# The feed-forward of a hybrid decoder layer: eight quarter products, or seven with sums and differences kept in DRAM

## The chip, the cores and the metric

The kernel runs on one core of a Trainium2 chip. The metric is the device time of one execution in microseconds. A core has five engines that each work through their own queue in order: TensorE (PE in the profile, with its weight loads as PEld), VectorE (DVE), ScalarE (ACT), GpSimd (POOL) and SyncE (SP). SP issues most DMAs, GpSimd a few. They meet through semaphores: an instruction that waits holds up all that stands behind it on its engine.

## What is computed

One layer on 2048 prompt tokens and 32 sample tokens, all in float32: an input projection, dilated attention and a gated branch, an output projection with norms, and then a feed-forward with a squared ReLU. The change is about the last part:

```python
x = x + rms_norm(merged @ w_out, norm_post_mix)
h2 = rms_norm(x, norm_pre_ffn)
f = jnp.square(jax.nn.relu(h2 @ w_up)) @ w_down      # 1024 -> 4096 -> 1024
x = x + rms_norm(f, norm_post_ffn)
```

## The kernel before

**Tokens.** The work is done in two spans, one after the other: span 0 has 1024 prompt and the 32 sample tokens (1056), span 1 has 1024. For each span the loop at the end of `hybrid_step` runs six projections with attention, `gmlp`, `mix`, the output projection (`out_and_norms` for span 0, `out_rows` for span 1) and `ffn`.

**Products.** A float32 number is held as two parts, high and low, in a format that TensorE takes at full rate. A product of two such numbers is three matrix instructions: high by high, high by low, low by high (L247 in `gemm`, L261 in `gemm_rows`). `load_w` fetches 512 KB of a weight from DRAM into `raw` (L218, on SP), ScalarE makes the high part (L234), GpSimd the low part by a subtraction (L237; every second one goes to VectorE while `share[0]` is set). The pool `wp` holds two buffers each of `raw`, `wh` and `wl`, so a weight's parts can be made once TensorE has done with the weight two before. The six 128-column weights of the first two attention steps are called weight 1 to 6 below, in the order in which their subtractions stand on GpSimd; 1 and 2 are q and k of the first step.

**Feed-forward.** `ffn` goes through the 32 row blocks of `w_up`: `up` makes one block for all tokens of the span, in tiles of 352 columns (span 0) or 512 (span 1), then ReLU on ScalarE, the square on VectorE, and the split in two parts. After each four blocks `down` or `down_rows` multiplies them by the matching part of `w_down` and VectorE adds the result to an accumulator in SBUF (L1106, L1118). For span 0 the tokens are the moving columns (352); for span 1 the weight is (256). The first four blocks use the shorter `late_chunks`, to begin before the last norms are done. Nothing of the feed-forward is kept in DRAM but its input rows `x1`.

**Order.** The program is written as one stream of matrix work; generators that are queued in `lanes` are moved on by `tick` between matrix instructions. A scheduler then sets each engine's order, with its own estimate of times; a generator's place in the source is therefore not where its instructions end up. Each DMA also waits for the one eight before it on its kind of queue (SP's, or GpSimd's), since eight completion semaphores are shared in turn.

Of the kernel before, what the change touches and what calls it, by code (L numbers as in the profile page):

```python
# [41 lines left out]
C_ALL = 832  # L42

# [29 lines left out]
def hybrid_step(ctx: ExitStack, tc: tile.TileContext, ins: dict, outs: list):  # L73
# [19 lines left out]
    wp = ctx.enter_context(tc.tile_pool(name="wp", bufs=2))  # L93
# [30 lines left out]
    b_gate = big.tile([P, 16], F32, name="b_gate")  # L124
    w_tril = big.tile([P, 4, P], F32, name="w_tril")
# [11 lines left out]
    x1_d = [dr.tile([SPAN_T[s], D], F32, name=f"x1_{s}") for s in range(2)]  # L137

# [10 lines left out]
    lanes = [deque(), deque(), deque()]  # L149
# [33 lines left out]
    def late_chunks(s):  # L183

        first = 512
        rest = SPAN_T[s] - first
        return [(0, first), (first, rest - 256), (first + rest - 256, 256)]
# [25 lines left out]
    def fetch_w(pieces):  # L213
        raw = wp.tile([P, 8 * P], F32, tag="raw", name="raw")
# [10 lines left out]
    def split_w(raw, o, into=None, early=False):  # L225
        if into is None:
            wh = wp.tile([P, 8 * P], F32R, tag="wh", name="wh")
            wl = wp.tile([P, 8 * P], F32R, tag="wl", name="wl")
        else:
            wh, wl = into[:, 0, :], into[:, 1, :]  # L230
# [8 lines left out]

    def gemm(w, offs, rhs, n, ticks=SLOW):  # L240

        pt = ps.tile([P, 512], F32, tag="g", bufs=3, name="pg")
# [10 lines left out]
    def gemm_rows(parts):  # L253

        pt = ps.tile([P, 512], F32, tag="g", bufs=3, name="pg")
# [28 lines left out]
    def to_channels(xt, n, c0, tag):  # L284

        for hf in range(2):
            pt = ps.tile([P, 512], F32, tag=tag, name="pt")
# [7 lines left out]
    def pre_mix(s, blks, gain, xts=None):  # L295
        for i, (c0, n) in enumerate(blks):
# [5 lines left out]
            junk = sm.tile([P, D], F32, tag="t", bufs=1, name="junk")  # L302
# [5 lines left out]
            to_channels(xt, n, c0, "t")  # L308
            yield

    def gain_rows(name):
        g = sm.tile([P, D], F32, tag="gbc", bufs=1, name="gbc")
        nc.sync.dma_start(g, ins[name].to_broadcast([P, D]))
        return g
# [30 lines left out]
    nc.sync.dma_start(b_gate, ins["b_gate"][0].rearrange("(k p) -> p k", p=P))  # L345
    nc.sync.dma_start(b_sp, ins["b_spatial"][0].unsqueeze(0).to_broadcast([P, 4, P]))
# [57 lines left out]
    def project(s, hp, g, idx):  # L404
# [42 lines left out]
        for i in (2,) if idx == 0 else (2, 0, 1):  # L447
# [34 lines left out]
    def attention(s, hp, g, idx, q, v):  # L482
# [51 lines left out]
        def scores(u):  # L534
# [3 lines left out]
            sp = ps.tile([P, 2, 2 * P], F32, tag="s", name="sp")  # L538
# [49 lines left out]
        def values(u):  # L588
# [4 lines left out]
            up = ps.tile([P, P], F32, tag="u", bufs=1, name="up")  # L593
# [87 lines left out]
    def sample_attention(hp):  # L681
# [104 lines left out]
        pl = ps.tile([P, 512], F32, tag="s", name="sp")  # L786
# [162 lines left out]

    def out_and_norms(s):  # L950
        gain = gain_rows("norm_post_mix")
        for j in range(4):
            new_slot(j, j < 2)
        gain2 = slots[2][:, :D]
        bufs = [slots[2][:, D : 2 * D], slots[3][:, :D], slots[3][:, D : 2 * D]]
        nc.sync.dma_start(gain2, ins["norm_pre_ffn"].to_broadcast([P, D]))
        used = [0]

        def norms(outT, c0, blks):
            def first(b0, bn):  # L960
                xt = sm.tile([P, D], F32, tag="x", name="xt")
                rows_io(s, b0, bn, xt, x_p, x_s, False)
                t = bufs[used[0] % 3]
# [8 lines left out]
                nc.vector.scalar_tensor_tensor(t[:bn], xt[:bn], rs[:bn], gain2[:bn], ALU.mult, ALU.mult)  # L972
# [3 lines left out]
            for blk in blks:  # L976
# [3 lines left out]
                if len(held) == 2:  # L980
                    to_channels(*held.popleft(), "s")
                    yield
            while held:
                to_channels(*held.popleft(), "s")
                yield
# [4 lines left out]
        gens = []  # L990
        for c0, n in late_chunks(s):
# [12 lines left out]
        return gens[1]  # L1004

    def out_rows(s):

        gain = gain_rows("norm_post_mix")
        for j in range(4):
            new_slot(j, j < 2)  # L1010
        gain2 = slots[2][:, :D]
        bufs = [slots[2][:, D : 2 * D], slots[3][:, :D], slots[3][:, D : 2 * D]]
        nc.sync.dma_start(gain2, ins["norm_pre_ffn"].to_broadcast([P, D]))
# [10 lines left out]
        def first(b):  # L1024
# [4 lines left out]
            nc.scalar.activation(bufs[b % 3], y, AF.Square, accum_out=ss)  # L1029
# [5 lines left out]
        def second(b):  # L1035
            y, t = rows[:, b, :], bufs[b % 3]
            ss = sm.tile([P, 1], F32, tag="ss", bufs=4, name="ss")
            nc.scalar.activation(t, y, AF.Square, accum_out=ss)
            rs = rstd_of(ss, P)
            nc.vector.scalar_tensor_tensor(t, y, rs, gain2, ALU.mult, ALU.mult)  # L1040
# [9 lines left out]
        def moved(b):  # L1050
            to_channels(bufs[b % 3], P, b * P, "s")
# [16 lines left out]
        for b in range(8):  # L1068
# [3 lines left out]
            if b >= 2:  # L1072
                ready = push(1, after(gens[b - 1], moved(b - 2)))
# [3 lines left out]
        return ready  # L1077

    def ffn(s, ready):
        place = (0, 1, 4, 5, 2, 3)  # L1080

        def up(f, spans):
            w = load_w([w_up[:, :, f * P : (f + 1) * P]])
            dst = pair(place[f % 6])
            for c0, n in spans:
                pt = gemm(w, K8, act_rhs(c0, n), n)
                r = sm.tile([P, 512], F32, tag="e0", name="relu")
                nc.scalar.activation(r[:, :n], pt, AF.Relu)  # L1088
                nc.vector.tensor_tensor(r[:, :n], r[:, :n], r[:, :n], ALU.mult)  # L1089
                split(dst[:, 0, c0 : c0 + n], dst[:, 1, c0 : c0 + n], r[:, :n], nc.gpsimd)  # L1090

        def down(fb, m2, spans):
            w = load_w([w_down[:, fb * 4 : fb * 4 + 4, m2 * 256 : m2 * 256 + 256]])
            for e in range(2):
                m = m2 * 2 + e
                for c0, n in spans:
                    def rhs(k):
                        f = pair(place[(fb * 4 + k) % 6])
                        return f[:, 0, c0 : c0 + n], f[:, 1, c0 : c0 + n]

                    pt = gemm(w, [k * 256 + e * P for k in range(4)], rhs, n)
                    acc = row(m)[:, c0 : c0 + n]
                    if fb == 0:
                        nc.vector.tensor_copy(acc, pt)
                    else:
                        nc.vector.tensor_tensor(acc, acc, pt, ALU.add)  # L1106

        def down_rows(fb, m2):
            wh, wl = load_w([w_down[:, fb * 4 : fb * 4 + 4, m2 * 256 : m2 * 256 + 256]])
            w = [(wh[:, k * 256 : (k + 1) * 256], wl[:, k * 256 : (k + 1) * 256]) for k in range(4)]  # L1110
            for b in range(0, 8, 2):
                pt = gemm_rows([(list(zip(lhs(fb, c), w)), 256) for c in (b, b + 1)])
                pt = pt.rearrange("p (b c) -> p b c", b=2)
                acc = yrows[:, b : b + 2, m2 * 256 : (m2 + 1) * 256]
                if fb == 0:
                    nc.vector.tensor_copy(acc, pt)
                else:
                    nc.vector.tensor_tensor(acc, acc, pt, ALU.add)  # L1118

        def lhs(fb, b):  # L1120
            fs = [pair(place[(fb * 4 + k) % 6]) for k in range(4)]
            return [(f[:, 0, b * P : (b + 1) * P], f[:, 1, b * P : (b + 1) * P]) for f in fs]
# [152 lines left out]
```

## Time and profile before

| | |
|---|---|
| median of 3 runs | 3090.62 us (3089.55 to 3097.53) |
| the profiled execution | 3089.51 us, span 3087.8 us, granted TensorE clock 0.996 |
| span 0: projections to output projection | from 0 to about 895 us |
| feed-forward of span 0 | about 895 to 1603 us |
| span 1: projections to output projection | about 1603 to 2372 us |
| feed-forward of span 1 | about 2372 us to the end |
| DMA | 238.76 MB, mean 77 GB/s |

The page gives busy time by engine, the chain of work that ended last (each step followed back to what released it), groups of instructions by source line, and the DMAs. Windows give the same for a stretch of the span. TensorE's matrix instructions overlap in the pipeline, so their spacing, not their duration, is what they cost.

### The profile page before, as it was taken

Reading aid. Unit: us, or ns where it says so; the run is one execution under the profiler, and the core shown is the slowest. Engines: PE = TensorE matmul, PEld = TensorE weight load, DVE = VectorE, ACT = ScalarE, POOL = GpSimd, SP = SyncE. Lnnn points to the kernel's source line nnn. Section 1 sums busy time; section 2 is a strip of 40 time slices with the busy share of each in tenths; the row PEclk is TensorE's granted clock in tenths of the full one; section 3 lists DMA queues with packets and bytes.
Section 4 is the critical chain, followed back from the end, with each engine's and each line's share of the span. In section 5 each row is a group of like instructions: output and inputs, shape, how many; then the busy total and the mean of one; then the engine's idle time right before and its main releaser. Section 6 shows DMA issues by size and latency. Waiting matters only on the chain.

```text
span 3087.8 us, 44446 instructions
## 1 busy us (share of the span) xinstructions
PE 3017.2 (98%) x18446; PEld 2799.4 (91%) x18446; DVE 1203.8 (39%) x2181; ACT 952.6 (31%) x1912; POOL 1062.1 (34%) x716
## 2 busy tenths in 40 slices
PE   8998989999999999999999999999999999999999
PEld 7997989998989999999998888788897988899998
DVE  5679774013652233332344354610127222222224
ACT  5443432113542112222135444521235222211113
POOL 2235254222443233333334232332335333333234
PEclk9999999999999999999999999999999999999999
DMA  4345441113431111111144222211134111111113
GB/s 139 106 124 150 135 119 46 45 50 96 154 103 44 46 49 46 44 49 48 42 129 135 82 79 80 65 45 50 45 94 152 55 49 48 49 42 48 48 48 117
DMA packets 324763, 238.76 MB, mean 77 GB/s; under 512 B 11600, under 2 KB 307088, under 8 KB 324560
## 3 DMA queue, kind: packets, MB, share of 16 engines
q1 hardware_dynamic: 321152, 232.44, 25.2%
q0 software_dynamic: 3264, 3.41, 0.5%
q8 instruction: 145, 2.38, 0.3%
q14 instruction: 58, 0.48, 0.1%
q10 hardware_dynamic: 144, 0.07, 0.0%
HBM read 201.17 MB, written 34.70 MB: 76 GB/s over the span
## 4 chain that ended last, share of the span: by engine, by line
PE 86%; DVE 6%; DMA 4%; issue 1%; ACT 1%; POOL 1%; SPq 0%; DVEq 0%; POOLq 0%; ACTq 0%
PE pg L247 66%; PE pg L261 15%; PE up L597 2%; DMA junk<-us 1%; PE pt L583 1%; DVE xt L769 1%; PE sp L549 1%; PE pt L290 1%; DMA us<-ov 1%; PE sp L550 1%; DVE ov L769 1%; DMA xt<-smp 1%; PE pt L936 0%; DVE relu L1089 0%; DVE junk L666 0%
## 5 line engine op out<-in xcount | busy, mean ns | idle before, releaser
L247 PE MATMUL pg<-act,wh 128*128 128x352 f32 (+3 forms) x6144 | 1676.1, 353 | 9.5 <-ACT ov L892 6.4
L247 PEld LDWEIGHTS pg<-act,wh 128*128 128x128 f32 x6144 | 1098.6, 189 | 117.6 <-ACT ov L892 6.7
L247 PE MATMUL pg<-act,wl 128*128 128x352 f32 (+3 forms) x3072 | 1083.1, 353 | 4.9 <-POOL wl L237 4.9
L237 POOL TENSOR_TENSOR wl<-raw,wh 128x1024 fp32r<-128x1024 f32 (+1 forms) x241 | 579.3, 2404 | 1193.9 <-ACT wh L234 1122.8
L247 PEld LDWEIGHTS pg<-act,wl 128*128 128x128 f32 x3072 | 580.3, 189 | 58.8 <-POOL wl L237 6.0
L234 ACT CAST wh<-raw 128x1024 fp32r<-128x1024 f32 (+1 forms) x248 | 256.6, 1035 | 986.8 <-PE pg L247 595.0
L1089 DVE TENSOR_TENSOR relu<-relu 128x352 f32<-128x352 f32 (+3 forms) x160 | 235.5, 1472 | 501.8 <-ACT relu L1088 501.8
L247 PE MATMUL pg<-pair,wh 128*128 128x352 f32 (+1 forms) x1376 | 342.3, 330 | 0.0
L261 PE MATMUL pg<-wh,pair 128*128 128x256 f32 x1280 | 255.3, 281 | 0.0
L247 PEld LDWEIGHTS pg<-pair,wh 128*128 128x128 f32 x1376 | 241.6, 188 | 5.7
L247 PE MATMUL pg<-pair,wl 128*128 128x352 f32 (+1 forms) x688 | 225.9, 328 | 0.0
L261 PEld LDWEIGHTS pg<-wh,pair 128*128 128x128 f32 x1280 | 210.1, 190 | 0.2
L261 PE MATMUL pg<-wl,pair 128*128 128x256 f32 x640 | 180.6, 282 | 0.0
L275 POOL TENSOR_TENSOR pair<-relu,pair 128x352 fp32r<-128x352 f32 (+2 forms) x110 | 119.8, 1090 | 175.6 <-ACT pair L274 175.6
L1106 DVE TENSOR_TENSOR ov<-ov,pg 128x352 f32<-128x352 f32 x168 | 86.6, 519 | 194.8 <-PE pg L247 194.7
L247 PE MATMUL pg<-oa,wh 128*128 128x352 f32 (+1 forms) x640 | 159.0, 329 | 0.0
L261 PE MATMUL pg<-wh,oa 128*128 128x256 f32 x640 | 143.6, 284 | 0.0
L1118 DVE TENSOR_TENSOR ov<-ov,pg 128x512 f32<-128x512 f32 x96 | 65.9, 686 | 191.8 <-PE pg L261 191.8
L555 ACT ACTIVATE ov<-ov 128x256 f32<-128x256 f32 (+1 forms) x192 | 91.8, 479 | 152.0 <-DVE ov L551 150.2
L920 DVE TENSOR_TENSOR xt<-xt,pg 128x352 f32<-128x352 f32 (+1 forms) x32 | 19.3, 604 | 302.5 <-ACT wh L234 141.0
L247 PEld LDWEIGHTS pg<-pair,wl 128*128 128x128 f32 x688 | 129.2, 188 | 3.0
L261 PEld LDWEIGHTS pg<-wl,pair 128*128 128x128 f32 x640 | 120.3, 188 | 0.2
(222 smaller groups left out, 3505.7 us busy)
## 6 DMA issues: line engine op xcount, KB each, us to landing
raw<-in_w_in_dram SPq DMA_DIRECT2D x84, 512.0 KB, 4.0
raw<-in_w_up_dram SPq DMA_DIRECT2D x72, 512.0 KB, 4.2
raw<-in_w_down_dram SPq DMA_DIRECT2D x64, 512.0 KB, 3.4
raw<-in_w_out_dram SPq DMA_DIRECT2D x24, 512.0 KB, 3.7
xt<-in_x_prompt_dram SPq DMA_DIRECT2D x23, 512.0 KB, 4.5
ov<-in_cache_kv_w_dram SPq DMA_DIRECT2D x44, 256.0 KB, 3.4
xt<-in_cache_kv_w_dram SPq DMA_DIRECT2D x28, 256.0 KB, 3.4
xt<-x SPq DMA_DIRECT2D x14, 512.0 KB, 3.6
```

Source lines behind the costliest of these rows:

```text
L234: nc.scalar.copy(wh[:, :o], raw[:, :o])
L237: eng.tensor_tensor(wl[:, :o], raw[:, :o], wh[:, :o].bitcast(F32), ALU.subtract)
L247: nc.tensor.matmul(pt[:, :n], a[:, o : o + P], b, start=(i == 0 and j == 0), stop=(i == last and j == 2))
L261: nc.tensor.matmul(pt[:, o : o + width], a, b, start=(i == 0 and j == 0), stop=(i == last and j == 2))
L275: eng.tensor_tensor(lo, src, h.bitcast(F32), ALU.subtract)
L290: nc.tensor.transpose(pt[:, j * P : j * P + n], xt[:n, k * P : (k + 1) * P], ident[:n, :n])
L555: nc.scalar.activation(pb[:, h, :w], pb[:, h, :w], AF.Exp, scale=-1.0, bias=uo[:, u, 128 + h : 129 + h], accum_out=uo[:, u, 130 + h : 131 ...
L597: nc.tensor.matmul(up[:, hs], tb[:, h, e * P : (e + 1) * P], vv[:, hs], start=(e == 0), stop=(e == len(rows) - 1),)
L769: nc.vector.tensor_tensor(pr.rearrange("p (t h d) -> p t h d", t=4, h=2), rows.rearrange("p t (h d) -> p t h d", h=2), sc4[:, :, :, key].u ...
L1089: nc.vector.tensor_tensor(r[:, :n], r[:, :n], r[:, :n], ALU.mult)
L1106: nc.vector.tensor_tensor(acc, acc, pt, ALU.add)
L1118: nc.vector.tensor_tensor(acc, acc, pt, ALU.add)
```

## The change

**Seven products.** Both feed-forward matrices and both operands are cut in quarters. A product of two 2 x 2 block matrices takes eight quarter products; here it takes seven, of the operands and of sums and differences of their quarters (Winograd's variant, with signs turned so that differences serve both stages). A table names, for each product, the form of the weight, the form of the activations, and which quarters of the result the product is added into:

```diff
+SEVEN = (
+    ("a11", "b11", ((X11, None),)),
+    ("s2", "v", ((X12, X11),)),
+    ("s3", "t3", ((X21, X12),)),
+    ("s1", "t1", ((X22, X21), (X12, X12))),
+    ("a12", "b21", ((X11, X11),)),
+    ("a22", "t4", ((X21, X21),)),
+    ("s4", "b22", ((X12, X12),)),
+)
```

**Weight sums.** The four sums s1 to s4 of the quarters of `w_up` and of `w_down` are made by DMA alone, from DRAM to DRAM: a copy on SP, then an adding DMA on GpSimd. There are 32 copies and 32 adds of 1 MB. They are a generator in a fourth lane, which `gemm` moves by one step on each third call:

```diff
+    def weight_sums():
+        for name, dst in (("w_up", up_d), ("w_down", down_d)):
...
+            for q in range(4):
...
+                for to, src in ((s1, a21), (s2, a11), (s3, a11), (s4, a12)):
+                    nc.sync.dma_start(to, src)
+                    yield
+                for to, src in ((s1, a22), (s3, a21), (s2, s1), (s4, s2)):
+                    nc.gpsimd.dma_start(to, src, accum_op=ALU.add, max_dma_last_dim=8192)
+                    yield
...
     def gemm(w, offs, rhs, n, ticks=SLOW):
+        calls[0] += 1
+        if calls[0] % 3 == 0:
+            step(3)
```

The push stands ahead of the loop over the spans: `push(3, weight_sums())`.

**Activations.** The normed input goes to DRAM, transposed and with its gain (`to_h2` in place of `to_channels`); `differences` reads it back, makes the four differences with four VectorE instructions (`differ`) and stores them. The result of the first matrix, squared, is stored with its differences in the same way, as seven forms per row block.

**Both spans at the end.** `ffn()` is called once, after span 1's output projection, and runs up and down for span 0, then for span 1. For span 0 a product has 528 columns, in two pieces of 264; for span 1 the moving side has 512 columns in both stages.

```diff
+        def mults(s, pt, w, x, first, last):
+            for j, (a, b) in enumerate(((0, 0), (0, 1), (1, 0))):
+                for c, n, o in pieces(s):
+                    nc.tensor.matmul(
+                        pt[:, o : o + n], w[:, a], x[:, b, c : c + n], start=first and j == 0, stop=last and j == 2
+                    )
...
+        def up(s, ops):
...
+            for u in range(16):
...
+                for p, (a, b, uses) in enumerate(SEVEN):
+                    w = next(ws)
+                    x = ops[b]
+                    pt = product_bank(s)
+                    for k in range(4):
+                        mults(s, pt, w[:, :, k], x[k], k == 0, k == 3)
...
+                    gather(result(s, pt), uses, X)
+                    for q in ((), (), (), (X22,), (X11,), (X21,), (X12,))[p]:
+                        nc.scalar.activation(X[q], X[q], AF.Relu, scale=1.0 if q in (X11, X12) else -1.0)
+                        nc.scalar.square(X[q], X[q])
...
+        def down(s, ring, X, aside):
...
+            for p, (a, b, uses) in enumerate(SEVEN):
...
+                for g in range(4):
+                    x += fill(ring[g], n, f_form(s, b, g))
+                for m in (0, 2):
+                    pts = [product_bank(s) for _ in range(2)]
+                    for k in range(0, 16, 2):
+                        w = next(ws)
+                        for i in range(2):
+                            for e in range(2):
+                                mults(s, pts[e], w[:, :, i, e * P : (e + 1) * P], x[k + i], k + i == 0, k + i == 15)
...
+                    for e in range(2):
+                        gather(result(s, pts[e]), uses, {q: X(q, m + e) for q in range(4)})
```

`fill` loads a form from DRAM in pairs of row blocks and splits it (ScalarE the high part, VectorE the low part). The weights come through `weight_stream`, two 128 x 512 pieces per fetch, with ScalarE and GpSimd making the parts. `down_rows` does the same as `down` for span 1, with the weight as the moving side. `gather` adds on VectorE from PSUM.

**Between the spans.** Since the feed-forward of span 0 no longer stands there, span 1's first norms (`pre_mix`) and its first q and k projection run beside the output projection of span 0, by its late chunks; that projection has a 512 and two 256 chunks in place of two 512. `wp` becomes one pool of six buffers, and the PSUM banks one tile of six whose banks are dealt out by kind.

**The order of the instructions, at the start on GpSimd.** Before, after the first two weights (the names are the source's; `flat` is a query buffer):

```order
L237 TENSOR_TENSOR wl<-raw,wh 128x1024 x2
L530 CAST oa<-flat_132 64x256 x6
L237 TENSOR_TENSOR wl<-raw,wh 128x1024
L530 CAST oa<-flat_132 64x256
L237 TENSOR_TENSOR wl<-raw,wh 128x1024
L360 AFFINE_SELECT w_tril<-w_tril 128x512
L237 TENSOR_TENSOR wl<-raw,wh 128x1024 x2
L530 CAST oa<-flat_132 64x256
```

In the changed kernel, at the same place, from the third subtraction to the fifth (seven adds stand ahead of these rows):

```order
L271 TENSOR_TENSOR wl<-raw,wh 128x1024
L1170 DMA up_sums<-in_w_up_dram 128x2048
L1170 DMA down_sums<-in_w_down_dram 512x512 x3
L1170 DMA up_sums<-up_sums 128x2048
L1170 DMA down_sums<-in_w_down_dram 512x512 x5
L1170 DMA up_sums<-up_sums 128x2048 x3
L271 TENSOR_TENSOR wl<-raw,wh 128x1024
L1170 DMA down_sums<-down_sums 128x2048 x2
L1170 DMA up_sums<-up_sums 128x2048
L597 CAST oa<-flat_143 64x256 x2
L1170 DMA down_sums<-down_sums 128x2048 x2
L1170 DMA up_sums<-up_sums 128x2048 x3
```

The last adds and the fifth to seventh subtraction follow at once, still on GpSimd; here with the semaphores that each instruction waits for (DMASW are the eight of GpSimd's own DMAs, DMAHW those of SP's):

```order
L271 TENSOR_TENSOR wl<-raw,wh 128x1024 [waits DMAHW5_49,Activation_49,Pool_49]
L1170 DMA down_sums<-down_sums 128x2048 [waits DMASW4_49]
L597 CAST oa<-flat_143 64x256 [waits PE_49,Pool_49]
L1170 DMA down_sums<-down_sums 128x2048 [waits DMAHW6_49,DMASW5_49]
L597 CAST oa<-flat_143 64x256 [waits PE_49]
L1170 DMA down_sums<-down_sums 128x2048 [waits DMAHW2_49,DMASW7_49,DMASW6_49]
L1170 DMA down_sums<-down_sums 128x2048 [waits DMAHW6_49,DMASW0_49]
L271 TENSOR_TENSOR wl<-raw,wh 128x1024 [waits DMAHW0_49,Activation_49,Pool_49]
```

So where four subtractions and some casts stood, all 32 adds now stand among them: 7 ahead of the third subtraction, 20 ahead of the fourth, 28 ahead of the fifth, 32 ahead of the sixth.

**At the start on SP.** Before, once the first token rows are issued:

```order
L355 DMA wsp<-in_w_spatial_dram 128x4x128
L710 DMA xt<-in_cache_kv_w_dram 128x4x128
L710 DMA ov<-in_cache_kv_w_dram 128x4x128
L218 DMA raw<-in_w_in_dram 128x8x128 x2
L805 DMA lnb<-in_ln_z_g_dram 128x512
L806 DMA lnb<-in_ln_z_b_dram 128x512
L218 DMA raw<-in_w_in_dram 128x8x128
```

In the changed kernel, there:

```order
L1167 DMA up_sums<-in_w_up_dram 128x2048 x3
L416 DMA wsp<-in_w_spatial_dram 128x4x128
L1167 DMA up_sums<-in_w_up_dram 128x2048
L777 DMA xt<-in_cache_kv_w_dram 128x4x128
L777 DMA ov<-in_cache_kv_w_dram 128x4x128
L1167 DMA up_sums<-in_w_up_dram 128x2048 x9
L252 DMA raw<-in_w_in_dram 128x8x128
L1167 DMA up_sums<-in_w_up_dram 128x2048 x3
L1167 DMA down_sums<-in_w_down_dram 512x512 x7
L872 DMA lnb<-in_ln_z_g_dram 128x512
L873 DMA lnb<-in_ln_z_b_dram 128x512
L1167 DMA down_sums<-in_w_down_dram 512x512 x9
```

All 32 copies have moved ahead of the fourth weight load, 13 of them ahead of the third.

More of the change, by code (lines that the diff above doesn't have):

```diff
@@ L1050, in moved @@
         def moved(b):
[L1051 removed]
+            to_h2(s, rows[:, b, :], P, b * P)
             yield
@@ L1228, in hybrid_step @@
         mix(s)
-        ready = out_rows(s) if s else out_and_norms(s)
-        ffn(s, ready)
+        if s == 0:
+            early = out_and_norms(s)
+        else:
+            out_rows(s)
+    ffn()
 _INS = [
```

515 lines of the change are left out of this document (362 added, 153 removed).

## The prediction

> **What bounds the kernel now.** I read the page first, for who is busy, then the chain of waits in order of time, for what one matrix instruction costs, and then the windows, for where a spare resource is.
>
> ```profile
> span 3087.8 us, 44446 instructions
> PE 3017.2 (98%) x18446; PEld 2799.4 (91%) x18446; DVE 1203.8 (39%) x2181; ACT 952.6 (31%) x1912; POOL 1062.1 (34%) x716
> PE 86%; DVE 6%; DMA 4%; issue 1%; ACT 1%; POOL 1%; SPq 0%; DVEq 0%; POOLq 0%; ACTq 0%
> ```
>
> TensorE is busy 98% of the span and carries 86% of the chain that ended last. Nothing else is above 39%. So matrix instructions that are taken away are worth their full spacing, as long as nothing makes TensorE wait. Their spacing stands in the chain of waits (start, length, what, how many):
>
> ```profile
> 894.66 649.46 PE pg L247 x4052
> ...
> 2422.37 46.29 PE pg L261 x384
> 2468.67 44.37 PE pg L247 x192
> ```
>
> In the feed-forward stages TensorE runs without a gap: 649.46/4052 = 160.3 ns for 352 columns, 46.29/384 = 120.5 ns for 256, 44.37/192 = 231.1 ns for 512. The columns set the price, so I can put a straight line through these points.
>
> The windows (busy time and count of PE, PEld, DVE, ACT, POOL, then granted clock, DMA share, GB/s) show the other resource that the change uses:
>
> ```profile
> 0.00:20.00 20.00, 7.27 (x29) 5.81 (x30) 12.47 (x21) 13.49 (x29) 6.98 (x8) 1.00 0.94 312
> 20.00:40.00 20.00, 18.24 (x140) 17.95 (x139) 16.01 (x25) 11.00 (x26) 3.74 (x5) 1.00 0.62 137
> 40.00:60.00 20.00, 19.10 (x147) 18.58 (x146) 10.21 (x28) 12.26 (x32) 6.75 (x6) 1.00 0.11 31
> 60.00:80.00 20.00, 20.00 (x130) 18.95 (x129) 1.24 (x9) 3.18 (x6) 2.40 (x1) 1.00 0.20 57
> 80.00:100.00 20.00, 19.47 (x133) 18.74 (x132) 10.98 (x25) 8.10 (x18) 4.03 (x3) 1.00 0.24 74
> 895.00:1544.00 649.00, 649.00 (x4053) 648.98 (x4052) 199.99 (x259) 136.18 (x229) 215.78 (x142) 1.00 0.16 47
> ```
>
> From 895 to 1544 us the DMA engines are 16% busy; only the first 20 us fill them (0.94). That row gives the rate of a full DMA system: 312/0.94 = 332 GB/s.
>
> **Part 1: the products.** Before, the feed-forward issues for span 0 4320 instructions of 352 columns (692.5 us) and, in the four late-chunk tiles, 96 each of 512, 288 and 256 columns (22.2 + 12.8 + 11.6 us; 288 by the line is 133.8 ns); for span 1 1536 of 512 (355.0) and 3072 of 256 (370.2). Sum 1464.3 us. After, span 0 has 16 x 7 x 4 x 3 x 2 = 2688 in the up stage and 7 x 2 x 16 x 2 x 3 x 2 = 2688 in the down stage, all of 264 columns. The line between 256 and 352 gives 120.5 + 8 x 0.415 = 123.8 ns, so 665.5 us. Span 1 has 1344 + 1344 of 512, 621.2 us. Sum 1286.7; with the 512-column chunk of the earlier projection split in two (+0.5) the change **takes 177 us from TensorE**. An eighth of 1464 would be 183: six of it go to the smaller piece of 264. What this needs beside TensorE:
>
> ```profile
> L1089 DVE TENSOR_TENSOR relu<-relu 128x512 f32<-128x512 f32 x68 | 111.9, 1645 | 258.2 <-ACT relu L1088 258.2
> L1118 DVE TENSOR_TENSOR ov<-ov,pg 128x512 f32<-128x512 f32 x96 | 65.9, 686 | 191.8 <-PE pg L261 191.8
> L237 POOL TENSOR_TENSOR wl<-raw,wh 128x1024 fp32r<-128x1024 f32 x225 | 549.2, 2442 | 1081.1 <-ACT wh L234 1017.3 <-issue 47.5 <-PE sp L549 4.1
> L237 DVE TENSOR_TENSOR wl<-raw,wh 128x1024 fp32r<-128x1024 f32 x9 | 17.7, 1965 | 6.8 <-ACT wh L234 6.7
> L234 ACT CAST wh<-raw 128x1024 fp32r<-128x1024 f32 x232 | 243.2, 1048 | 932.2 <-PE pg L247 540.4 <-PE pg L261 263.2 <-issue 116.9
> L1088 ACT ACTIVATE relu<-pg 128x512 f32<-128x512 f32 x68 | 40.4, 594 | 55.5 <-PE pg L247 55.5
> ```
>
> One row block of the up stage takes TensorE 168 x 123.8 = 20.8 us. In it VectorE has seven sums out of PSUM (0.69) and four differences (at most 1.65): 11.4 us. ScalarE has seven half-size weight casts (0.52) and nine passes (0.59): 9.0. GpSimd has seven half-size subtractions (1.22): 8.5. The DMA moves 1.84 MB of weights and 1.89 MB of forms, 179 GB/s against 332. All fit under TensorE. In the order of the changed kernel a weight pair's load stands four products (11.9 us) ahead of its use. A down product has 47.5 us for eight form fills of 1.05 (cast) + 1.97 (subtraction) us. So inside the stages I cost this at nothing; if the cover fails, rival 3 prices it.
>
> At the four hand-overs (into up and down of each span) operands must land, be cast and be split before their places are used. Below, the gap of before at 840 to 895 goes (48.73 of 55 us busy): -6. Above, each waits once for all of it, 4 x (4.2 + 1.05 + 1.97) = 29.
>
> ```profile
> 840.00:895.00 55.00, 48.73 (x311) 44.25 (x311) 33.55 (x39) 27.04 (x58) 27.12 (x16) 0.97 0.43 135
> ```
>
> The page's list of DMAs gives the median time to landing at the end of its rows:
>
> ```profile
> raw<-in_w_up_dram SPq DMA_DIRECT2D x72, 512.0 KB, 4.2
> raw<-in_w_down_dram SPq DMA_DIRECT2D x64, 512.0 KB, 3.4
> ...
> out_dram<-xt SPq DMA_DIRECT2D x13, 512.0 KB, 2.9
> ```
>
> Of the two ends I take **+8**, nearer the low one, since the first two or more operands are filled before each stage starts. The squares, the norms and the transposes only move, with TensorE work of out_rows and of the next projection beside them.
>
> **Part 2: the weight sums.** This is where I expect the change to be decided. Lane 3 looks as if it spread 64 DMAs of 1.05 MB over span 0, one each third product. The order shows otherwise: all 32 copies stand on SP before the fourth weight load, and all 32 adds on GpSimd before the sixth weight subtraction. An add waits for its copy and for the add eight before it, and behind it on GpSimd stand subtractions 3 to 6 and the query casts; TensorE's third instruction with a weight waits for its subtraction. SP's third weight load has 13 copies ahead of it.
>
> ```profile
> 53.76 2.39 POOL L237 TENSOR_TENSOR wl<-raw,wh 128x1024 fp32r<-128x1024 f32 x1 [6.32 <-ACT wh L234]
> ...
> 81.75 2.37 POOL L237 TENSOR_TENSOR wl<-raw,wh 128x1024 fp32r<-128x1024 f32 x1 [10.85 <-ACT wh L234]
> ...
> 98.82 2.78 POOL L237 TENSOR_TENSOR wl<-raw,wh 128x1024 fp32r<-128x1024 f32 x1 [14.16 <-ACT wh L234]
> ```
>
> Before (GpSimd's timeline), subtraction 3 ran at 53.8 us, 6 at 81.8 and 7 at 98.8, when weight 5 gave its buffer free. TensorE's work with weight 6 begins there in the chain of waits:
>
> ```profile
> 97.06 2.73 PE pg L247 x17
> ```
>  After, subtraction 6 stands behind add 32, whose issue needs add 25 landed. By then the DMA engines have moved 32 copies, 25 adds and the 12.2 MB of the first 100 us (20 us each of 312, 137, 31, 57 and 74 GB/s), the last in 37 us. Until then TensorE has only weights 3 to 5 and their attention to run, which took it some 40 us (55 to 97) before; its queue is in order.
>
> No row shows a transfer from DRAM to DRAM or one that adds. A copy costs at least what a load of 1.05 MB costs at 332 GB/s, 3.16 us, and at most twice that, 6.3, if its read and its write share that rate. I take the middle, 4.74: loads and stores appear apart in the rows, and nothing there says which end is nearer. An add has one read more than a copy: at least 3.16 if that read and the write are hidden, at most 3 x 3.16 = 9.5; I take 4.74 + 3.16 = 7.9. Weight 6 then starts at 37 + 32 x 4.74 + 25 x 7.9 + 2.4 = 388.6 us: **a delay of 291 us**, between 122 (all at 3.16) and 382 (6.3 and 9.5). The last seven adds still share the DMA with the weight loads that follow: nothing, or their whole 55 us less some 12 us of TensorE's own work with weight 6 (72 x 160.3 ns); I take **+15**. That nothing is gained elsewhere I take from TensorE's 98%: what is late at 100 us stays late.
>
> [...]
>
> **The sum**, against the profiled execution (3089.5 us, 1.1 below the median 3090.62): 3089.5 - 177 + 291 + 8 + 15 = 3227, 4.4% slower.
>
> **Rivals.**
> 1. The transfers are as cheap as loads and the change wins. For it: 332 GB/s was reached with reads and a store of 512 KB lands in 2.9 us, a load in 3.4 to 4.2. Against it: those rows use one side of DRAM at a time. All 57 at 3.16 us give a delay of 122: 3089.5 - 177 + 122 + 8 = 3043. It decides in its favour where the delay is under 154 us, that is 57 transfers in 211 us, 3.70 us each.
> 2. An add costs two copies, since both of its reads go through the same reading side. With 9.5 us for an add: 37 + 152 + 237 + 2.4 - 97 = 331, total 3267; with the copy at its upper end too, 382, total 3318. [...] No row here can say.
> 3. The change does not do what it says: the products wait for operands. Each of 14 form sets of the down stages waits once for landing, cast and subtraction, 3.4 + 1.05 + 1.97 = 6.4 us: 90 more, 3317. For it: one ring of places serves two products. Against it: a place is free a whole pass ahead.
> 4. The adds do not hold TensorE at all, and the 177 us stay: 3089.5 - 177 + 8 = 2920. It needs 57 transfers of 1.05 MB in the first 80 us, 750 GB/s, over twice the fullest row.
>
> **How the numbers follow.** The forecast, 3150 to 3300 by price, has 0.42; dearer adds (rival 2) 0.25; waits in the products 0.05; cheap transfers (rival 1) 0.18; rival 4 0.03; a middle between forecast and rival 1 (3081 to 3150) 0.07. A measurement tells 0.3% (9 us) from no change. Faster by more: 0.18 + 0.03 = 0.21. Within: 0.04 of the middle. Slower: 0.42 + 0.25 + 0.05 + 0.03 = 0.75. The range goes from 3030 (all at 3.16 and the old gap gone: 3089.5 - 177 + 122 - 6) to 3318 (both upper ends); it leaves out rival 4 and the tails of rivals 2 and 3.
>
> **What would show it.** Right: the DMA share near 1 from 20 us to some 440 us, TensorE almost idle between about 60 and 390 us, GpSimd's subtractions 3 to 6 late and released after L1170, the software queue with some 33 MB, and then feed-forward stages without gaps: about 665 us for L1307 at 264 columns. Wrong: the sixth subtraction before 250 us (rival 1), TensorE under 95% busy inside the down stages (rival 3), or columns of 264 that cost more than 124 ns each.

## The result: 37% slower

The changed kernel takes 4236.84 us (4223.81 to 4243.57, 4 runs), the kernel before 3093.19 in the same comparison: a ratio of 1.369, 95% interval 1.365 to 1.373. The forecast was 3227, the range ended at 3318. The direction was right, the size was short by 1010 us. The profiled execution of after took 4233.09 us.

The head of its page, against 98% for TensorE before:

```profile
span 4231.3 us, 44914 instructions
PE 3267.4 (77%) x17350; PEld 2761.6 (65%) x17350; DVE 1272.7 (30%) x2292; ACT 1252.5 (30%) x2302; POOL 1171.7 (28%) x900
```

TensorE does 1096 instructions less than before (17350, not 18446), is busy for 250 us more, and idle for 964 us where it had been idle for 71. So instructions were saved, each got dearer, and TensorE waits. The windows of after (PE, PEld, DVE, ACT, POOL, then granted clock, DMA share, GB/s) show where:

```profile
0.00:100.00 100.00, 44.78 (x286) 40.80 (x286) 34.22 (x63) 29.08 (x66) 17.84 (x20) 0.78 0.99 286
100.00:200.00 100.00, 15.85 (x81) 14.18 (x81) 1.43 (x3) 2.86 (x5) 10.07 (x9) 0.59 1.04 259
200.00:300.00 100.00, 41.40 (x170) 34.73 (x171) 22.24 (x55) 16.55 (x40) 23.20 (x24) 0.62 0.98 211
300.00:850.00 550.00, 398.77 (x1895) 348.58 (x1894) 266.17 (x626) 139.56 (x373) 120.11 (x113) 0.79 0.31 88
850.00:1300.00 450.00, 373.50 (x2122) 336.89 (x2122) 83.50 (x158) 95.89 (x150) 105.69 (x74) 1.00 0.15 44
3200.00:3300.00 100.00, 93.36 (x738) 92.61 (x737) 29.06 (x27) 35.05 (x46) 38.67 (x29) 0.97 0.52 167
```

The first three rows are the weight sums that the prediction spoke of: DMA engines full, TensorE a third busy. But the two rows behind them are stages that the change was not thought to touch, with the DMA at 15 to 31% and no engine above 83%. Before, TensorE was 94 to 96% busy in these stages:

```profile
97.00:400.00 303.00, 284.43 (x1926) 275.63 (x1924) 240.25 (x581) 128.96 (x369) 111.95 (x94) 0.98 0.46 133
700.00:895.00 195.00, 188.08 (x1201) 173.29 (x1201) 103.28 (x143) 92.64 (x190) 72.66 (x37) 0.99 0.42 129
```

What TensorE waits for stands in the view of waits (tile and line, releaser; us in total, times, longest):

```profile
PE banks L1307 <- DVE ov L1316: 200.0, 194, 4.0
PE banks L286 <- ACT wh L268: 158.1, 3, 125.1
PE banks L616 <- DVE ov L618: 67.5, 81, 6.7
PE banks L286 <- DVE pair L489: 63.1, 22, 8.2
PE banks L286 <- ACT xt L979: 47.9, 64, 2.3
```

Only the second row is a late weight. The others are readers of PSUM: VectorE's `gather` in the products, the masks behind the scores, the split of the keys, the sigmoids of the gates. Before, the largest wait of this kind was 11.6 us in 9 times (the masks). TensorE's timeline in the gate stage (start, length, name, count, idle time before it and its releaser):

```profile
1011.64 0.59 PE L286 MATMUL banks<-act,wh 128*128 128x352 f32 x2 [0.61 <-DVE junk L989]
1016.45 0.59 PE L286 MATMUL banks<-act,wh 128*128 128x352 f32 x2 [0.64 <-ACT xt L979]
1021.20 0.59 PE L286 MATMUL banks<-act,wh 128*128 128x352 f32 x2 [0.64 <-ACT xt L979]
1026.07 0.59 PE L286 MATMUL banks<-act,wh 128*128 128x352 f32 x2 [0.70 <-ACT junk L979]
1030.87 0.59 PE L286 MATMUL banks<-act,wh 128*128 128x352 f32 x2 [0.64 <-ACT xt L979]
```

Each group of 24 matmuls starts after a gap that ends with a reader. The program as built says which: here, for the first matmul of a group in the gate stage, the reader on ScalarE that it waits for, and the last matmul that this reader waits for itself (numbers count along each engine).

```
changed: PE 2728 into banks    waits ACT 430 (L979), which reads what PE 2704 to 2727 wrote
changed: PE 2752 into banks    waits ACT 431 (L979), which reads what PE 2728 to 2751 wrote
apart:   PE 2725 into bg_5002  waits ACT 420 (L978), which reads bg_4895, PE 2644 to 2667
apart:   PE 2757 into bg_5028  waits ACT 421 (L978), which reads bg_4932, PE 2668 to 2696
```

In the changed kernel a group waits for the reader of the group **just before it**, though that one lies in another of the six banks. With a tile for each bank ("apart", the first experiment) it waits for the reader of the group three back, which has long been done. The six banks are there, and dealt out in turn; but they are slices of one tile, and the waits that the framework puts in follow the tile.

**Theory A** then is: the one tile costs the missing 1000 us, in gaps and in a lower granted clock. **Theory B**: the weight sums and late weights are the larger part, and the PSUM waits only stand where something else is late. **Theory C**: the feed-forward part is bound by its stream from DRAM.

### The profile page after: what moved, and what is told of

Same layout as the page of the kernel before. It is cut to its first block, busy times and chain, and to the rows that moved or that the text cites. A ratio compares the mean times of both kernels' runs of the same rounds, so it can differ in the third digit from the quotient of the medians.

```text
span 4231.3 us, 44914 instructions
## 1 busy us (share of the span) xinstructions
PE 3267.4 (77%) x17350; PEld 2761.6 (65%) x17350; DVE 1272.7 (30%) x2292; ACT 1252.5 (30%) x2302; POOL 1171.7 (28%) x900
## 5 line engine op out<-in xcount | busy, mean ns | idle before, releaser
L286 PE MATMUL banks<-act,wh 128*128 128x352 f32 (+3 forms) x3616 | 1082.8, 384 | 381.9 <-ACT wh L268 158.1
L286 PEld LDWEIGHTS banks<-act,wh 128*128 128x128 f32 x3616 | 697.4, 210 | 514.4 <-ACT wh L268 159.0
L1220 POOL TENSOR_TENSOR wf<-raw,wf 128x512 fp32r<-128x512 f32 x448 | 592.4, 1332 | 1008.5 <-ACT wf L1219 717.1
L286 PE MATMUL banks<-act,wl 128*128 128x352 f32 (+3 forms) x1808 | 675.3, 374 | 5.7 <-POOL wl L271 5.1
L1307 PE MATMUL banks<-act,wf 128*128 128x264 f32 (+1 forms) x3648 | 568.8, 313 | 122.2 <-DVE ov L1316 97.4
L1307 PEld LDWEIGHTS banks<-act,wf 128*128 128x128 f32 x3648 | 498.4, 190 | 190.0 <-DVE ov L1316 92.5
L271 POOL TENSOR_TENSOR wl<-raw,wh 128x1024 fp32r<-128x1024 f32 (+1 forms) x112 | 258.8, 2311 | 1067.6 <-PE banks L286 835.2
L1219 ACT CAST wf<-raw 128x512 fp32r<-128x512 f32 x448 | 277.0, 619 | 878.2 <-DMA raw<-up_sums 251.5
L286 PEld LDWEIGHTS banks<-act,wl 128*128 128x128 f32 x1808 | 378.6, 209 | 41.4 <-POOL wl L271 6.3
L1307 PE MATMUL banks<-pair,wf 128*128 128x264 f32 (+1 forms) x1824 | 285.0, 312 | 57.7 <-DVE ov L1316 55.2
L1387 PEld LDWEIGHTS banks<-wf,act 128*128 128x128 f32 x1008 | 194.8, 195 | 83.0 <-issue 13.1
```

The costliest lines, as they stand in the source:

```text
L271: eng.tensor_tensor(wl[:, :o], raw[:, :o], wh[:, :o].bitcast(F32), ALU.subtract)
L286: nc.tensor.matmul(pt[:, :n], a[:, o : o + P], b, start=(i == 0 and j == 0), stop=(i == last and j == 2))
L1219: nc.scalar.copy(high, raw)
L1220: eng.tensor_tensor(low, raw, high.bitcast(F32), ALU.subtract)
L1307: nc.tensor.matmul(pt[:, o : o + n], w[:, a], x[:, b, c : c + n], start=first and j == 0, stop=last and j == 2)
L1387: nc.tensor.matmul(pts[t], x[k][:, c, t * P : (t + 1) * P], w[:, d, 0], start=k == 0 and j == 0, stop=k == 15 and j == 2)
```

## The experiments

All ratios are to the kernel before, run beside them (3093.7 to 3095.9 us).

**1. The banks as tiles of their own.** A PSUM pool with the kinds of before, closed ahead of `ffn` for three tiles of two banks, and these for six of one ahead of span 1's products:

```diff
-    banks = ps.tile([P, 6 * 512], F32, name="banks", bufs=1)
...
-        return banks[:, i * 512 : (i + 1) * 512]
+        return psx.tile([P, 512], F32, tag=kind, bufs=n, name="b" + kind)
...
-                return banks[:, i % 3 * 1024 : (i % 3 + 1) * 1024]
-            return banks[:, i % 6 * 512 : (i % 6 + 1) * 512]
+                return psf.tile([P, 1024], F32, tag="f", bufs=3, name="pf")
+            return psh.tile([P, 512], F32, tag="f", bufs=6, name="ph")
```

> The changed kernel with one edit: the six PSUM banks that the change holds as one tile are tiles of their own again (three of kind g, two of kind s, one of kind u ahead of the feed-forward part, as before the change; in it three tiles of two banks for span 0 and six of one for span 1). Theory A (one tile makes each group of matmuls wait for the reader of the group just before it, and the gaps lower the granted clock): after its profile the stages ahead of the feed-forward part lose about 610 us (the 2476 us until the feed-forward part begins, less 1663 before the change and about 200 of the delay by the weight sums), and the feed-forward part falls from 1755 to 1300 to 1450: 3250 us (3150 to 3450). Theory B (the weight sums' transfers and late weights in the shared pool are the larger part, the PSUM waits only stand where something else is late anyway): over 3900 us. Theory C (the feed-forward part is bound by its stream from DRAM): about 3600, with the feed-forward part still near 1700.

Measured: 3240.01 us, ratio 1.048 (1.045 to 1.050). The one edit gives back 997 us, 10 us below what theory A said; B falls, and so does C: from the first product to the end it takes 1350 us, where after took 1669. The scheduler sets the order anew for each program (in the rows above, the groups of "apart" begin 32 matmuls apart and not 24, since other matrix work stands between them), so the 997 us hold what the new order brings as well; no run keeps the order still. Its page:

```profile
span 3228.3 us, 44867 instructions
PE 2892.7 (90%) x17350; PEld 2619.2 (81%) x17350; DVE 1303.3 (40%) x2292; ACT 1225.4 (38%) x2304; POOL 1190.2 (37%) x900
```

TensorE runs the same 17350 instructions, with 628 us less idle time (336 for 964) and 375 us less busy time. The second part shows in the groups by form (busy us, mean ns of one, idle before); first the row of after, then that of this run:

```profile
L286 PE MATMUL banks<-act,wh 128*128 128x352 f32 x1920 | 534.9, 363 | 274.2 <-ACT wh L268 158.1 <-DVE pair L489 29.3 <-ACT xt L979 22.2
```

```profile
L285 PE MATMUL bg<-act,wh 128*128 128x352 f32 x1920 | 494.0, 338 | 173.3 <-ACT wh L267 168.0 <-ACT ov L958 3.3 <-DVE flat L172 1.9
```

Nearly all the idle time that is left here is the late weight of the sums (168.0); the readers are down to a few us.

**2. The one tile, put into the kernel before.** Nothing else of the change:

```diff
+    banks = ps.tile([P, 6 * 512], F32, name="banks", bufs=1)
...
-        pt = ps.tile([P, 512], F32, tag="g", bufs=3, name="pg")
+        pt = bank("g")
...
-            sp = ps.tile([P, 2, 2 * P], F32, tag="s", name="sp")
+            sp = bank("s").rearrange("p (h k) -> p h k", h=2)
```

> The kernel before the change with only this edit: its six PSUM tiles of kinds g, s and u are slices of one tile, dealt out by kind as in the changed kernel. Theory A: the same stages lose the same 610 us, and the 400 or so groups of 24 matmuls of the old feed-forward part lose 0.6 to 1.4 us each: 3950 us (3700 to 4250), with the granted clock down to 0.7 to 0.9 in the attention stages. Theory B: within 60 us of 3090, the clock at 0.97 or more.

Measured: 4444.47 us, ratio 1.436 (1.431 to 1.440). The edit alone makes the old kernel slower than the whole change did: 1349 us, more than in the changed kernel, and 194 us over the upper end of the expectation. What was put too low there are the stages ahead of the feed-forward parts, at 610 us. The feed-forward parts lost 520 us, within what was expected of them: in span 0 from the first ReLU to the last accumulating add 1042 us for 753, in span 1 from the first ReLU to the end 957 for 726. The other 845 of the 1365 us between the two profiled runs lie in the stages ahead of each. A stretch of the feed-forward part of span 0, and the first waits:

```profile
1400.00:2200.00 800.00, 640.19 (x3613) 575.07 (x3612) 168.75 (x226) 122.98 (x203) 191.07 (x127) 1.00 0.11 33
```

```profile
PE banks L256 <- ACT relu L1097: 144.9, 149, 1.8
PE banks L256 <- DVE ov L1115: 103.9, 163, 1.4
PE banks L270 <- DVE ov L1127: 71.3, 90, 0.9
```

Where TensorE ran without a gap before, it is 80% busy, with ReLU and the accumulating add as releasers, at 0.6 to 1 us each.

**3. Three tiles of two banks**, each with one bank of kind g and one of s or u; all else as changed:

```diff
-    banks = ps.tile([P, 6 * 512], F32, name="banks", bufs=1)
+    pairs = [ps.tile([P, 2 * 512], F32, tag=f"b{i}", name=f"banks{i}", bufs=1) for i in range(3)]
...
```

> The changed kernel with its six PSUM banks as three tiles of two banks (each of kind g with one of kind s or u) instead of one tile of six, all else as changed, the weight sums hoisted as there. Theory A: only groups that share a pair wait for each other's readers; products and gate groups, which take the three in turn, hardly: 3240 us of the run with banks apart plus 0 to 150: 3300. If it were the number of banks or the sharing by kinds as such: over 3700.

Measured: 3322.15 us, ratio 1.074 (1.072 to 1.076). As many banks, dealt out in turn by kind as before, and 915 us gained; the pairs still cost 82 against tiles of their own. The size of the tile sets the wait, not the number of banks.

**4. The weight sums, put into the kernel before**, as 64 transfers whose results nothing uses:

```diff
...
+    push(3, weight_sums())
     idx = 0
     merges = {}
```

> The kernel before the change with only the 64 transfers of the weight sums (32 copies on SP, 32 adds on GpSimd) added, their results used by nothing. Theory A: only the delay at the start, about 200 us (150 to 300): 3290 us (3240 to 3390). Theory B: the transfers also make the weights of later stages late, 500 us or more: over 3600. My prediction's term would give 3381.

Measured: 3271.80 us, ratio 1.057 (1.055 to 1.059): 177 us for the sums.

**5. The changed kernel without the sums**, with the banks apart and with the one tile. The sum forms are read from quarters of the weights, so the products are others than the reference's:

```diff
-    push(3, weight_sums())
...
-            src = down_d[SUMS.index(form), k * P : (k + nk) * P, m : m + nm]
+            i, j = divmod(SUMS.index(form), 2)
+            src = ins["w_down"][0][j * 2048 + k * P : j * 2048 + (k + nk) * P, i * 512 + m : i * 512 + m + nm]
```

> The changed kernel with the PSUM banks as tiles of their own and without the 64 transfers of the weight sums; the four sum forms are read from quarters of the weights instead, so the products are not those of the reference, but as many of the same shape and with the same bytes streamed. Theory A: the time of the run with banks apart less about 200: 3050 us (2920 to 3250). Theory B with only the sums to blame: over 3300 us as the PSUM edit brings nothing. Theory C: about 3400, the feed-forward part still near 1700.

> The changed kernel, its six banks one tile as there, without the 64 transfers of the weight sums (the four sum forms are read from quarters of the weights, so the products are not those of the reference). If the delay by the sums and the waits of the one tile add up: 4237 less the 206 us between the runs with banks apart with and without sums, 4030 us (3990 to 4070). If groups that wait for readers leave slack in which the transfers pass: over 4130.

Measured: apart 3034.39 us, ratio 0.980 (0.979 to 0.982); one tile 4068.26, ratio 1.314 (1.310 to 1.318). The sums cost 206 us with the banks apart and 169 with the one tile: the two terms add up but for 37 us. Without both of them the seven products win, by 61 us, though not with the layer's values.

**6. The sums paced**, with the banks apart. Each transfer is kept behind the last weight load (SP) or subtraction (GpSimd) on its own queue, from the 15th weight on:

```diff
-        calls[0] += 1
-        if calls[0] % 3 == 0:
-            step(3)
...
+        loads[0] += 1
+        if loads[0] > 14:
+            step(3)
...
-                    nc.sync.dma_start(to, src)
+                    behind(nc.sync.dma_start(to, src), "SP")
...
```

> The changed kernel with the banks apart and the weight sums paced: from the 15th weight on, each weight that is loaded lets one of the 64 transfers go, a copy queued on SP behind the last weight's load, an add on GpSimd behind its last subtraction; the values are those of the reference. Theory S (the sums cost time only because the scheduler hoists them ahead of the first stage's weights): the run without sums (3034 us) and little more for shared bandwidth: 3050 us (3030 to 3090), TensorE as busy in the first 400 us as without them. Rival T (67 MB through the DMA cost their time wherever they stand): 3150 or more.

Measured: 3053.64 us, ratio 0.987 (0.985 to 0.989). The same 67 MB cost 19 us over the run without them (3034.39), instead of 206. Its first windows, beside the first three rows of after above:

```profile
0.00:100.00 100.00, 85.86 (x587) 81.81 (x588) 54.11 (x110) 50.04 (x116) 27.68 (x25) 1.00 0.42 122
100.00:200.00 100.00, 99.13 (x690) 97.12 (x689) 66.22 (x175) 45.12 (x128) 21.95 (x21) 1.00 0.46 136
```

**7. What is left of the loss.** The paced kernel stands well above 3089.5 - 177 + 8 = 2920, the prediction's sum without the sums. Two places show it: TensorE waits 43.6 us for the transposes behind span 0's output product, and in the last down stage its matrix instructions wait 13.1 us for weight parts. (A third, 30.0 us behind the masks of the scores where it was 11.6 before, was not followed up.) For the first place: three buffers for the norms instead of two, and the reverse edit in the kernel before.

```diff
-                t = bufs[used[0] % 2]
+                t = bufs[used[0] % 3] if used[0] % 3 < 2 else spare()
```

> The paced kernel, and the norms behind span 0's output product take turns at three buffers again (two halves of a slot, and a tile of the weight pool) instead of the two that the change leaves. Theory U (with two buffers and two blocks held the next block waits for the transposes of the block before, 42 us of waits at the transposes of that stage): 40 us less than the paced kernel (20 to 60). Rival V (the stage is long because the next span's norms were moved into it and share ScalarE and VectorE): within 10 us of the paced kernel.

> The kernel before the change with one edit: the norms behind span 0's output product take turns at two buffers instead of three. Theory U: 40 us more (20 to 60). Rival V: within 10 us of 3090.

Measured: 3055.41 us (ratio 0.988, 0.986 to 0.989), no gain over 3053.64; the kernel before with two buffers 3094.58 (1.000, 0.999 to 1.001). Theory U falls: the buffers are not it.

For the second place, the stream fetched one raw tile ahead, the weight pool parted as before:

```diff
-            raw, _ = fetch_w(two)
+            raw, _ = ahead
+            ahead = fetch_w(srcs[i + 2 : i + 4]) if i + 2 < len(srcs) else None
...
```

> The paced kernel with the weight pool parted again into two raw tiles and four of parts, and the feed-forward part's stream fetching each raw tile one ahead. Theory W (in the last down stage the raw tile is fetched only when the one before is split, which leaves 31.6 us of TensorE waiting for parts there): 25 us less than the paced kernel (10 to 40). Rival X (the splitting on GpSimd at 1.3 us a part sets that stage's pace): within 10 us of it.

Measured: **3023.14 us, ratio 0.977 (0.976 to 0.979)**, 30.5 us under the paced kernel. What ended TensorE's idle time in that stage (us, times), in the paced kernel and then with the stream ahead; this view adds the matrix instructions and their weight loads, which run beside each other (in the second window above 99.13 and 97.12 us busy of 100):

```profile
  POOL wf L1225: 19.8, 13
  ACT wf L1224: 11.0, 5
```

```profile
  POOL wf L1225: 9.5, 6
  ACT wf L1224: 1.5, 2
```

Of these, the matrix instructions alone wait 8.3 + 4.8 us in the paced kernel and 4.1 + 0.5 with the stream ahead (the expectation's 31.6 us, too, counts both kinds). The profiled runs lie 26 us apart: 14 of them are in this stage (from its first product to the end 349.3 and 335.3 us), 9.5 in the products of span 0 (676.7 and 667.2), which have the same stream. GpSimd's pace, the rival, is not the bound. How much of the gain is the parted pool's was not tried by itself. This version leaves nothing of the layer out, and it is the fastest here that doesn't.

For the first place again, on this kernel: the next span's norms and transposes left out (theory V), and one block more held, with the three buffers of above, so that the transposes come later (theory U2).

```diff
-            early.append((ready, m, push(1, pre_mix(s + 1, blocks(s + 1, ready, m), gain_next, None, spare))))
+            early.append((ready, m, push(1, iter(()))))
```

```diff
-                if len(held) == 2:
+                if len(held) == 3:
```

> The kernel of the stream ahead without the next span's norms and transposes beside span 0's output product (the second span's projections then read what the mixing left, so its values are not the reference's; the work behind them is the same). Theory V (that stage is long because the next span's norms were moved into it, where the change left only the output product to cover them; before they ran beside the feed-forward part): the 42.9 us of waits at the stage's transposes, some 10 us of transposes and a few us of lower clock go: 2970 us (2950 to 2990). Rival U2 (span 0's own chain of norms holds TensorE there, whatever runs beside it): 3005 or more.

> The kernel of the stream ahead with three buffers for span 0's norms and three blocks held, so that a block's transposes stand one block later in TensorE's order. Theory U2 (the transposes stand too early in TensorE's order for the chain of norms behind them): 25 us less than the stream ahead (10 to 45), 2998. Theory V: within 10 us of 3023.

Measured: without the next span's norms 2949.22 us (ratio 0.954, 0.952 to 0.955), 74 us less; with three held 3036.11 (0.982, 0.980 to 0.983), 13 us more. U2 falls. V has the right sign and about the size, though both runs lie just outside what it said (2950 to 2990, and within 10 us of 3023). The wait for the transposes and the windows of that stage, with the stream ahead:

```profile
PE bs L341 <- DVE flat L1043: 42.9, 6, 9.8
```

```profile
800.00:850.00 50.00, 26.54 (x162) 25.13 (x163) 22.31 (x37) 16.88 (x39) 8.86 (x5) 0.70 0.70 188
850.00:900.00 50.00, 35.92 (x245) 35.47 (x244) 21.63 (x39) 20.00 (x43) 13.19 (x7) 0.81 0.76 229
```

The same without the next span's norms:

```profile
PE bs L341 <- DVE flat L1043: 7.8, 2, 5.7
```

```profile
800.00:850.00 50.00, 44.28 (x347) 44.08 (x346) 22.98 (x46) 20.82 (x49) 19.11 (x10) 0.93 1.07 325
850.00:900.00 50.00, 45.34 (x285) 40.11 (x284) 26.77 (x46) 19.62 (x47) 23.88 (x17) 0.97 0.95 245
```

Neither VectorE nor ScalarE is half busy in the slow windows. The likely reading, which no run shows step by step, is that two chains of norms take turns on them and TensorE waits for the one that comes last. The clock is lower with it (0.70 and 0.81).

The three terms together (30.5, 74 and the 19 that the paced sums still cost) leave some 10 us of the distance to 2920 open.

## Why the prediction failed

**The step that failed** is Part 1's "All fit under TensorE ... So inside the stages I cost this at nothing". It compared busy times of engines and the bytes of the DMA, but not how long a group's result holds its place in PSUM. The change's section had named it, "the PSUM banks one tile of six whose banks are dealt out by kind", and the prediction gave it no term. The orders that were read were GpSimd's and SP's, not the waits in TensorE's own. The one tile costs 997 us, all but 13 of the 1010 us that were missing, and not only in the feed-forward part: the prediction took the stages ahead of it as unchanged, and there stand two thirds of it: the first product starts at 2562.0 us in after and at 1878.6 with the banks apart.

**The weight sums**: right in mechanism, too dear. The delay and its tail were put at 291 + 15 us; the runs show 206, 169 and 177. After's GpSimd timeline gives the price; in its first row here an add ends 15.70 us in which GpSimd waits for that add's copy and runs nothing that stands behind it:

```profile
53.99 0.81 POOL L1170 DMA_DIRECT2D up_sums<-in_w_up_dram  x1 [15.70 <-DMA up_sums<-in_w_up_dram]
...
101.47 2.35 POOL L271 TENSOR_TENSOR wl<-raw,wh 128x1024 fp32r<-128x1024 f32 x1 [1.55 <-ACT wh L268]
...
277.82 1.65 POOL L1170 DMA_DIRECT2D down_sums<-down_sums  x2
293.72 2.37 POOL L271 TENSOR_TENSOR wl<-raw,wh 128x1024 fp32r<-128x1024 f32 x1 [14.25 <-issue]
```

The sixth subtraction was forecast for 386 us and ran at 293.7. By the prediction's own count of 57 transfers behind 37 us of other traffic that is (293.7 - 37)/57 = 4.5 us each, copies and adds together, and that is an upper end: the last two adds were issued at 277.8 us, which gives 4.2, and what held the subtraction for the 14 us behind them the profile doesn't say. It ends at 296.1 us, 199 later than the 97 at which the work with weight 6 began before, close to the 206, 169 and 177 of the runs. The page's rows of the DMA queues (packets, MB, share of 16 engines' span) tell the two apart, since the runs with the banks apart with and without the sums differ by 32 copies on q1 and 32 adds on q0. With them:

```profile
q1 hardware_dynamic: 463376, 470.34, 46.5%
q0 software_dynamic: 10944, 36.97, 5.8%
```

Without them:

```profile
q1 hardware_dynamic: 452624, 436.79, 45.9%
q0 software_dynamic: 3264, 3.41, 0.5%
```

Of q1, 46.5% of 3228.3 less 45.9% of 3028.2 is 111 us: 3.5 us a copy. Of q0, 5.8% less 0.5% likewise is 172 us: 5.4 us an add, an estimate each, as the other transfers on q1 also land later in the crowd: 256 KB of the cache (`ov`) in 31.8 us (median of 3) in the first 300 us of after, in 2.9 (of 41) between 300 and 1300. The prediction had 4.74 and 7.9. Rival 2 (9.5 for an add, a delay of 331 us) falls by both numbers. An add costs 5.4/3.5 = 1.5 copies, by these estimates. Rival 1 needed 3.70 us or less for a transfer on average, and there were 4.2 to 4.5. Rival 4 (the adds hold nobody) comes close only when they are paced: 19 us.

**The products**: right. With the banks apart 48 products of 264 columns start 5.84 us before the next 24, 121.7 ns each (each lasts 285 ns on average, so they overlap), against 123.8 forecast:

```profile
1907.17 6.01 PE L1306 MATMUL pf<-act,wf 128*128 128x264 f32 x48
1913.01 3.09 PE L1306 MATMUL pf<-pair,wf 128*128 128x264 f32 x24
```

Span 0's products run there from 1878.6 to 2556.4 us, 678 for a forecast of 665.5. In after that stage shows what the prediction had named as the sign of rival 3, TensorE under 95% (93.36 in the window at 3200); the mechanism was another one. That the format of the two parts is the fast one shows in before: 512 columns cost 231.1 ns in it (44.37/192), and the 512 of L785, one product in plain float32, run as two passes that begin some 0.43 us apart (1.02 less the 0.59 of one):

```profile
276.58 1.02 PE L785 MATMUL pt<-xt,con 128*8 128x512 f32 x2 [2.36 <-DVE e L664]
```

**"The squares, the norms and the transposes only move"**: wrong by up to 74 us. Span 1's norms had run beside the feed-forward of span 0. Where they stand now there is only the output product to cover them. (Some of the 74 is the transposes' own time on TensorE, which any place would cost.)

**Waits for operands** (rival 3, put at 90 us): not as it said. No wait at the products of the paced kernel is for a set of forms. What came late there were the weights' parts: fetching them earlier gained 30.5 us, about half of it in the last down stage.

Put together for the kernel with the banks apart: 3227 - 100 (sums) + 74 (norms) + 30 (stream) = 3231, and 3240 was measured. That the forecast lies 13 us beside that run is luck: an error of 100 us on each side. The 997 us then come on top.

## What to carry to other kernels

Slices of one tile are not buffers: before counting on overlap, read in the built program which earlier instruction the first matmul of a group waits for, on TensorE itself and not only on the engines that were changed. Work without dependencies does not stay where it is written; one added dependency for each, on the stream of its own queue, made 64 transfers cost 19 us instead of 206. When a stage is moved, ask what had run in its cover, and what covers that now.

## What was unexpected of the hardware

The granted clock did not follow TensorE's idle share. In after's window 850 to 1300 TensorE was idle for 17% of the time, the longest of the listed waits was 2.4 us, and the clock stayed at 1.00. From 300 to 850 it was idle for 27%, with waits of up to 6.9 us, and the clock fell to 0.79:

```profile
PE banks L286 <- ACT xt L979: 22.2, 32, 2.3
...
PE banks L286 <- ACT ov L170: 4.0, 2, 2.4
```

```profile
PE banks L616 <- DVE ov L618: 40.9, 38, 6.7
PE banks L286 <- DVE pair L489: 29.3, 10, 6.9
```

After's record of the clock holds 1 or one half, and every spell in it, but the one that the end of the run cuts, lasts a multiple of 3.41 us. In the first of these windows none of some hundred gaps of TensorE was longer than 2.4 us, and the clock stayed; in the second ten were above 3.41 us, and it fell to one half 27 times. In a third window TensorE was idle for 19%:

```profile
1600.00:2000.00 400.00, 324.69 (x1340) 249.42 (x1339) 95.98 (x314) 115.55 (x278) 59.65 (x74) 0.81 0.17 47
```

The clock fell to one half 17 times there, and only one gap was above 3.41 us (8.2), so the falls do not go with the number of such gaps. No run here tried the length of a gap by itself; what sets the clock stays open.

Dealing the banks out in turn was not enough to let the reader of one group run beside the next: it was done in after and in experiments 1 to 3 alike, and the time went from 4237 (one tile) to 3322 (three) to 3240 us (a tile for each bank) with the size of the tile.
